# Sums made by accumulating transfers instead of by GpSimd and VectorE

## The chip, the cores and the metric

The kernel runs on one core of a Trainium2 chip. The metric is the device time of one execution in microseconds, the median of several runs. The engines are TensorE (PE in the profile; its weight loads PEld), VectorE (DVE), ScalarE (ACT), GpSimd (POOL) and SyncE (SP); the last three also issue transfers (DMA), each on a queue of its own that runs in order. Matrix products go from SBUF to PSUM; the other engines take them from PSUM.

## The reference

One inference step of a one-layer streaming encoder with 1024 prompt tokens and 64 sample tokens, model width 1024, all in float32:

```python
xn = rms_norm(x, g_attn)
rq, rk, rv, rg, sq, sk, sv, ga, gb = split(xn @ w_in)
A = rms_norm(retention(rope(rq), rope(rk), rv)) * silu(rg) @ w_ret_out
B = sliding_window_attention(sq, sk, sv, bias, sinks) @ w_swa_out
x += (sigmoid(ga) * A + sigmoid(gb) * B) @ w_mix_out
x += cross_attention(rms_norm(x, g_cross), memory)
x += (silu(rms_norm(x, g_ffn) @ w_gate) * (rms_norm(x, g_ffn) @ w_up)) @ w_down
y = rms_norm(x, g_final)
```

Three pieces matter here. The token norms need, for each of 1088 tokens, the sum of squares over 1024 features. The rotary turn makes from two halves a, b of a head the rows a cos - b sin and b cos + a sin. And nearly all large products are formed by Strassen's scheme in Winograd's form.

## The kernel before

**Layout.** Activations lie with features on the 128 partitions and the 1088 tokens along the row, in two halves of 544. Each float32 operand is split in two parts (a rounded one by a ScalarE cast, L125, the remainder by a VectorE subtraction, L126), and a product takes three matmuls (high x high, high x low, low x high).

**Strassen.** `strassen` (L270) makes a two by two block product of two weight tiles with the activations: seven products P1, P2, P6, P5, P7, P3, P4 in that order on TensorE. Each product is 4 x 6 matmuls of 272 columns (3 x 6 where a weight tile has only 384 rows). Between them VectorE adds up what is common to several results (u2, u5, u3), and `emit` takes each of the four results. The call with `part` (last group of the down projection) leaves out P2 and P4; these are made by `finish` with the rest weights.

**Weights.** For each step a pair of raw tiles is loaded by SP (tag raw, one pair of buffers in all), and `weight_ops` (L169) makes seven operands of them: P1 = a11, P2 = a12, P7 = a11 - a21, P6 = a22 - P7, P5 = a21 + a22, P3 = a12 - P6, P4 = a22. The four sums are made in place in the raw tiles, on GpSimd (L186, L187, L189, L192), on VectorE in five steps of the down projection (`by`). Each operand is split into a weight buffer (tag wq): five of them during the projections, six later. A weight buffer comes free when its product is done; the raw tiles come free when P3 and P4 are split, and only then can SP load the next pair.

**Order.** The products follow one another on TensorE; a planner with a simulated timeline puts the instructions of every engine in order, except where `issue_after` or `in_order` binds them. Each engine and each DMA queue then runs its own list in order.

**Stages.** (1) Projections, to about 800 us: 27 Strassen steps after two plain products; between the products the steps of the retention run. `rotated` turns a head of queries or keys in emit (four multiplications with cos and sin on VectorE, two additions per half of the tokens, on VectorE for the first two heads, on GpSimd for the others), then stores it. `token_squares` (L517) loads the 16 half tiles of x again, squares them on ScalarE and adds them on VectorE (L528) into the row `rstd`; `token_roots` needs the result at the third step of the next key product. (2) Window attention, merging and cross attention, to about 1480 us. (3) Gate and up products, 21 Strassen steps. (4) Down projection in three groups of 6, 8 and 8 feature tiles; each group goes over the eight output tiles in pairs m = 0, 2, 4, 6; `add` (L1739) adds the results to y, the part from PSUM on VectorE (L1742), the part from SBUF on GpSimd or, in the five steps with `turns`, on VectorE (L1744). While a group ends, the operands of the next are loaded (hl, from d_op) and split. In the last group's last step the eight halves of the rest weights (`hr`) are loaded too. (5) `finish`: the rest products, the final norm and the stores.

## Time and profile before

| | before |
|---|---|
| median of 3 runs | 2199.45 us (2199.18 to 2199.67) |
| profiled execution | 2199.31 us |
| its span | 2197.5 us |
| TensorE busy | 2155.3 us, 98% |
| VectorE busy | 1596.9 us, 73% |
| ScalarE busy | 884.3 us, 40% |
| GpSimd busy | 649.6 us, 30% |
| moved by DMA | 291.86 MB |

All times in the profile are microseconds from the start of the span, unless marked ns. A group's row gives line, engine, operation, tiles (written <- read), shape and count, then the busy time in us and the mean of one in ns, then the idle time of the engine just before these instructions with what ended it. A row of a DMA group ends with the median time from issue to landing. A timeline row gives start, duration, engine, line and operation.

### The profile page before, as it was taken

To read this page: it belongs to the slowest core of one execution; us is meant where nothing else is said; L and a number is where in the kernel's file an instruction comes from. 1 tells how busy PE (TensorE), PEld (TensorE's weight loads), DVE (VectorE), ACT (ScalarE), POOL (GpSimd) and SP (SyncE) were. 2 spreads that over 40 slices of the span, in tenths; PEclk is the share of its full clock that TensorE was granted. 3 is DMA by queue.
4 is the path that set the end of the run, shared out by engine and by line. 5 is a ranking of instruction groups with operands and counts; after the bars stand their busy time and mean duration, and the time that the engine had idled before them with its cause. 6 is when DMAs were issued, how large, how long until landed. Compare 5 with 4: busy or idle time off the path is not lost.

```text
span 2197.5 us, 41612 instructions
## 1 busy us (share of the span) xinstructions
PE 2155.3 (98%) x16388; PEld 2104.3 (96%) x16388; DVE 1596.9 (73%) x2721; ACT 884.3 (40%) x1902; POOL 649.6 (30%) x484
## 2 busy tenths in 40 slices
PE   9999999999999998999999999999999999999988
PEld 9999999999999997889999999999999999999987
DVE  7798878767688668876545555768877767779776
ACT  6434343437444355653233433343223222335433
POOL 2224535352264112320000000016655555431121
PEclk9999999999999999999999999999999999999999
DMA  4533434343455485427443121413433232466332
GB/s 172 185 110 111 149 111 162 121 138 112 136 187 163 143 272 161 134 77 231 129 150 112 40 73 55 140 57 109 146 114 104 96 119 81 150 231 221 111 116 82
DMA packets 160981, 291.86 MB, mean 133 GB/s; under 512 B 21554, under 2 KB 90098, under 8 KB 160658
## 3 DMA queue, kind: packets, MB, share of 16 engines
q1 hardware_dynamic: 151074, 263.42, 37.1%
q0 software_dynamic: 5104, 17.44, 2.2%
q10 hardware_dynamic: 4608, 8.36, 1.0%
q8 instruction: 129, 2.11, 0.4%
q14 instruction: 66, 0.54, 0.1%
HBM read 197.99 MB, written 91.95 MB: 132 GB/s over the span
## 4 chain that ended last, share of the span: by engine, by line
PE 74%; DVE 12%; DMA 6%; issue 3%; ACT 3%; POOL 2%; SPq 0%; DVEq 0%; ACTq 0%; POOLq 0%
PE pq L208 14%; PE pq L211 13%; PE pq L209 13%; PE pd L152 7%; PE pd L154 7%; PE pd L153 7%; DVE wq L126 3%; PE pss L1168 1%; DVE stage L659 1%; DVE B L126 1%; DMA hl<-d_op 1%; DMA raw<-w_down 1%; ACT wq L125 1%; DVE u L277 1%; DMA qs<-d_qkv 1%
## 5 line engine op out<-in xcount | busy, mean ns | idle before, releaser
L126 DVE TENSOR_TENSOR wq<-raw,wq 128x512 fp32r<-128x512 f32 (+1 forms) x498 | 444.8, 899 | 159.4 <-ACT wq L125 157.5
L125 ACT CAST wq<-raw 128x512 fp32r<-128x512 f32 (+1 forms) x498 | 299.6, 612 | 567.3 <-PE pq L211 210.6
L208 PE MATMUL pq<-T,wq 128*128 128x272 f32 x1800 | 496.8, 294 | 13.9 <-ACT wq L125 9.6
L209 PE MATMUL pq<-T,wq 128*128 128x272 f32 x1800 | 491.2, 289 | 0.0
L208 PE MATMUL pq<-B,wq 128*128 128x272 f32 x1550 | 424.3, 292 | 0.5 <-DVE u L277 0.5
L209 PE MATMUL pq<-B,wq 128*128 128x272 f32 x1550 | 420.0, 288 | 1.1 <-DVE B L126 1.1
L211 PE MATMUL pq<-T,wq 128*128 128x272 f32 x1800 | 374.6, 289 | 0.0
L186 POOL TENSOR_TENSOR raw<-raw 128x512 f32<-128x512 f32 (+1 forms) x53 | 79.1, 1493 | 996.1 <-DVE rs_r L316 477.1
L208 PEld LDWEIGHTS pq<-T,wq 128*128 128x128 f32 x1800 | 341.8, 190 | 17.0 <-ACT wq L125 10.3
L209 PEld LDWEIGHTS pq<-T,wq 128*128 128x128 f32 x1800 | 345.1, 192 | 0.0
L211 PE MATMUL pq<-B,wq 128*128 128x272 f32 x1550 | 320.3, 287 | 0.0
L209 PEld LDWEIGHTS pq<-B,wq 128*128 128x128 f32 x1550 | 294.5, 190 | 1.3 <-DVE B L126 1.3
L208 PEld LDWEIGHTS pq<-B,wq 128*128 128x128 f32 x1550 | 291.6, 188 | 1.6 <-issue 1.4
L211 PEld LDWEIGHTS pq<-T,wq 128*128 128x128 f32 x1800 | 281.7, 190 | 0.2
L211 PEld LDWEIGHTS pq<-B,wq 128*128 128x128 f32 x1550 | 240.2, 188 | 0.0
L277 DVE TENSOR_TENSOR u<-pq,u 128x544 f32<-128x544 f32 x174 | 125.1, 719 | 64.7 <-PE pq L211 64.0
L189 POOL TENSOR_TENSOR raw<-raw 128x512 f32<-128x512 f32 (+1 forms) x53 | 75.3, 1421 | 95.5 <-DVE wq L126 91.3
L659 DVE TENSOR_TENSOR stage<-pq,u 128x544 f32<-128x544 f32 x108 | 77.5, 717 | 32.5 <-PE pq L211 21.5
L1196 POOL TENSOR_TENSOR t<-t,den 128x768 f32<-128x768 f32 (+2 forms) x34 | 49.6, 1460 | 126.7 <-DVE den L1194 40.3
L192 POOL TENSOR_TENSOR raw<-raw 128x512 f32<-128x512 f32 (+1 forms) x53 | 76.9, 1452 | 15.6 <-DVE wq L126 12.2
L187 POOL TENSOR_TENSOR raw<-raw 128x512 f32<-128x512 f32 (+1 forms) x53 | 78.1, 1474 | 3.4
L152 PE MATMUL pd<-xc,wq 128*128 128x256 f32 (+1 forms) x256 | 74.6, 291 | 0.3 <-DVE qf L1453 0.3
(411 smaller groups left out, 4742.3 us busy)
## 6 DMA issues: line engine op xcount, KB each, us to landing
hl<-d_op SPq DMA_DIRECT2D x84, 272.0 KB, 4.2
d_op<-stage SPq DMA_DIRECT2D x44, 272.0 KB, 2.3
d_op<-ht SPq DMA_DIRECT2D x44, 272.0 KB, 4.2
raw<-w_gate SPq DMA_DIRECT2D x22, 512.0 KB, 3.5
raw<-w_up SPq DMA_DIRECT2D x22, 512.0 KB, 4.9
raw<-w_down SPq DMA_DIRECT2D x16, 512.0 KB, 4.2
d_gate<-stage ACTq DMA_DIRECT2D x28, 272.0 KB, 2.5
d_qkv<-stage SPq DMA_DIRECT2D x24, 272.0 KB, 2.9
```

Source lines behind the costliest of these rows:

```text
L125: self.last_cast = self.nc.scalar.copy(hi, src).ins
L126: self.last_low = self.nc.vector.tensor_tensor(out=lo, in0=src, in1=hi.bitcast(F32), op=ALU.subtract).ins
L152: mm(ps, wh, xh, start=start, stop=False)
L153: mm(ps, wh, xl, start=False, stop=False)
L154: self.last_mm = mm(ps, wl, xh, start=False, stop=stop).ins
L186: tt(out=a11, in0=a11, in1=a21, op=sub)
L187: tt(out=a21, in0=a21, in1=a22, op=add)
L208: mm(ps[:, c, :HC], w[:, 0, ks], x[:, 0, cs], start=start, stop=False)
L209: mm(ps[:, c, :HC], w[:, 0, ks], x[:, 1, cs], start=False, stop=False)
L211: self.last_mm = mm(ps[:, c, :HC], w[:, 1, ks], x[:, 0, c * HC:(c + 1) * HC], start=False, stop=stop).ins
L277: add = lambda out, a, b: nc.vector.tensor_tensor(out=out, in0=a, in1=b, op=ALU.add)
L659: nc.vector.tensor_tensor(out=o, in0=ps, in1=sb, op=ALU.add)
```

## The change

1. `weight_ops`: the four sums of a step become transfers that add to their target, issued by GpSimd (`dma_start` with `accum_op`). Such a transfer can only add, so the operands change sign where the scheme subtracts: P7 = a11 + a21, P6 = P7 + a22, P5 as before, P3 = a12 + P6, and the sums behind the products subtract instead (`join` with a sign). This holds for all steps, so `by` goes.
2. `token_squares`: the additions become accumulating transfers, and the loop takes the two halves of the tokens in turn for each tile instead of one half after the other.
3. `rotated`: b sin is formed with its sign turned, and both additions become accumulating transfers, for all heads.
4. `add` of the down projection: all additions to y on VectorE.
5. The loads of the rest weights are bound behind the last load of the last pair of weights.

```diff
-        tt = (by or nc.gpsimd).tensor_tensor
+        def plus(out, x):
+            self.last_sum = nc.gpsimd.dma_start(out, x, accum_op=ALU.add).ins
+
         put("P1", a11)
         put("P2", a12)
-        tt(out=a11, in0=a11, in1=a21, op=sub)
-        tt(out=a21, in0=a21, in1=a22, op=add)
+        plus(a11, a21)
+        plus(a21, a22)
         put("P7", a11)
-        tt(out=a11, in0=a22, in1=a11, op=sub)
+        plus(a11, a22)
         put("P6", a11)
         put("P5", a21)
-        self.last_sum = tt(out=a12, in0=a12, in1=a11, op=sub).ins
+        plus(a12, a11)
         put("P3", a12)
         put("P4", a22)
...
-        add(u2, self.product(w, x, "P6", "T2"), u1)
-        add(u5, self.product(w, x, "P5", "T1"), u2)
+        self.join(u2, self.product(w, x, "P6", "T2"), u1, "b-p")
+        self.join(u5, self.product(w, x, "P5", "T1"), u2, "p-b")
         ps = self.product(w, x, "P7", "T3")
-        add(u3, ps, u2)
-        emit(1, 1, ps, u5)
-        emit(0, 1, self.product(w, x, "P3", "B22"), u5)
-        emit(1, 0, None if part else self.product(w, x, "P4", "T4"), u3)
+        self.join(u3, ps, u2)
+        emit(1, 1, ps, u5, "b-p")
+        emit(0, 1, self.product(w, x, "P3", "B22"), u5, "p-b")
+        emit(1, 0, None if part else self.product(w, x, "P4", "T4"), u3, "p-b")
+
+    def join(self, out, ps, sb, signs="p+b"):
+        a, b = (sb, ps) if signs == "b-p" else (ps, sb)
+        self.nc.vector.tensor_tensor(out=out, in0=a, in1=b, op=ALU.add if signs == "p+b" else ALU.subtract)
...
-        for t in range(2):
-            hs = slice(t * HALF, (t + 1) * HALF)
-            for k in range(KT):
-                x = self.ra.tile([P, HALF], F32, tag=tags[k % 4], bufs=1, name="xsq")
+        for k in range(KT):
+            for t in range(2):
+                hs = slice(t * HALF, (t + 1) * HALF)
+                x = self.ra.tile([P, HALF], F32, tag=tags[(2 * k + t) % 4], bufs=1, name="xsq")
                 self.load(x, self.io["xT"][k, :, hs])
                 acc = self.rstd[:, hs]
                 nc.scalar.activation(x if k else acc, x, AF.Square)
                 if k:
-                    nc.vector.tensor_tensor(out=acc, in0=acc, in1=x, op=ALU.add)
+                    nc.gpsimd.dma_start(acc, x, accum_op=ALU.add)
...
-                    tt(out=sb, in0=b, in1=sin, op=ALU.mult)
+                    nc.vector.scalar_tensor_tensor(sb, b, -1.0, sin, ALU.mult, ALU.mult)
                     tt(out=sa, in0=a, in1=sin, op=ALU.mult)
                     tt(out=a, in0=a, in1=cos, op=ALU.mult)
+                    nc.gpsimd.dma_start(a, sb, accum_op=ALU.add)
                     tt(out=b, in0=b, in1=cos, op=ALU.mult)
-                    add = (nc.vector if h < 2 else nc.gpsimd).tensor_tensor
-                    add(out=a, in0=a, in1=sb, op=ALU.subtract)
-                    add(out=b, in0=b, in1=sa, op=ALU.add)
+                    nc.gpsimd.dma_start(b, sa, accum_op=ALU.add)
...
             if ps is not None:
-                nc.vector.tensor_tensor(out=v, in0=ps, in1=v, op=ALU.add)
+                self.join(v, ps, v, "b-p" if signs == "b-p" else "p+b")
             if sb is not None:
-                by.tensor_tensor(out=v, in0=sb, in1=v, op=ALU.add)
+                self.join(v, v, sb, "p-b" if signs == "p-b" else "p+b")
...
                 if last and m == KT - 2:
                     rest_raws = []
-                    for i in range(KT):
-                        pool = self.more if i < 6 else self.hl
-                        rest_raws.append(pool.tile([P, HALF], F32, tag="hl", name="hr")[:, :n])
-                        load_half(rest_raws[i], i, f0 + g // 2, f0 + g)
+                    with self.tc.issue_after(self.loaded):
+                        for i in range(KT):
+                            pool = self.more if i < 6 else self.hl
+                            rest_raws.append(pool.tile([P, HALF], F32, tag="hl", name="hr")[:, :n])
+                            load_half(rest_raws[i], i, f0 + g // 2, f0 + g)
...
-                    w = self.weight_ops(raws, n, ("P2", "P4") if last else (), by)
+                    w = self.weight_ops(raws, n, ("P2", "P4") if last else ())
```

More of the change, by code (lines that the diff above doesn't have):

```diff
@@ L276, in strassen @@
         u1, u2, u3, u5 = (self.fp.tile([P, 2, HC], F32, tag=t, bufs=1, name=t) for t in ("u1", "u2", "u3", "u5"))
-        add = lambda out, a, b: nc.vector.tensor_tensor(out=out, in0=a, in1=b, op=ALU.add)
         ps = self.product(w, x, "P1", "B11")
@@ L658, in taken, with emit @@
                 else:
[L659 removed]
+                    self.join(o, ps, sb, signs)
                 return flat(o)
             def project(w, put, act=None, other=None):
[L663 to L664 removed]
+                def emit(i, t, ps, sb, signs="p+b"):
+                    o = taken(ps, sb, signs)
                     (nc.vector if act is not None else nc.gpsimd).tensor_tensor(
@@ L702, in values, with emit @@
             def values(w, h, by=self.strassen):
-                def emit(i, t, ps, sb):
-                    self.store(self.d_qkv[2, 2 * h + i, :, half(t)], taken(ps, sb))
+                def emit(i, t, ps, sb, signs="p+b"):
+                    self.store(self.d_qkv[2, 2 * h + i, :, half(t)], taken(ps, sb, signs))
                 by(w, self.ops, emit)
@@ L714, in emit @@
                         left.extend((2, 2))
-                    o, r = taken(ps, sb), self.rstd[:, half(t)]
+                    o, r = taken(ps, sb, signs), self.rstd[:, half(t)]
                     at, edge = (slice(0, 512), slice(512, HALF)) if t == 0 else (slice(32, HALF), slice(0, 32))
@@ L1647, in save, with gate @@
                 self.store(self.d_op[OPS.index(name), n], src)
-            def gate(i, t, ps, sb):
+            def gate(i, t, ps, sb, signs="p+b"):
                 g = gates[i, t]
                 if sb is not None:
-                    nc.vector.tensor_tensor(out=g, in0=ps, in1=sb, op=ALU.add)
+                    self.join(g, ps, sb, signs)
                     ps = None
@@ L1758, in load_half @@
         def load_half(tile, m, a, b):
-            self.load(tile.rearrange("p (k m) -> p k m", m=P), io["w_down"][m, :, a:b, :])
+            self.loaded = self.load(tile.rearrange("p (k m) -> p k m", m=P), io["w_down"][m, :, a:b, :])
         for gi, g in enumerate(GROUPS):
@@ L1764, in down, with emit @@
             for m in range(0, KT, 2):
-                turns = m == KT - 2 and not last or m in (0, 2) and gi > 0
-                by = nc.vector if turns else nc.gpsimd
-                def emit(i, t, ps, sb, m=m, by=by):
-                    add(m, i, t, ps, sb, by)
+                def emit(i, t, ps, sb, signs="p+b", m=m):
+                    add(m, i, t, ps, sb, signs)
                     if last and t == 1:
```

20 lines of the change are left out of this document (8 added, 12 removed).

## The prediction

> **What bounds the kernel now.** I read the page's first part, then a table of busy time by stretch, then the waits and the chain at the places where TensorE stands still.
>
> ```profile
> span 2197.5 us, 41612 instructions
> PE 2155.3 (98%) x16388; PEld 2104.3 (96%) x16388; DVE 1596.9 (73%) x2721; ACT 884.3 (40%) x1902; POOL 649.6 (30%) x484
> ```
>
> TensorE is busy for 98% of the span: 2197.5 - 2155.3 = 42.2 us is all that can be saved by feeding it better, apart from time at a lower clock. By stretch (start:end, length, busy time and count of each engine, granted clock, DMA share, GB/s):
>
> ```profile
> 70.00:120.00 50.00, 47.08 (x360) 46.64 (x359) 47.35 (x67) 20.96 (x36) 13.06 (x8) 0.96 0.52 171
> 800.00:900.00 100.00, 90.46 (x677) 74.69 (x675) 84.47 (x201) 62.77 (x225) 25.42 (x21) 0.98 0.60 189
> 1480.00:1920.00 440.00, 440.00 (x3507) 440.00 (x3506) 335.03 (x393) 132.94 (x225) 247.03 (x164) 1.00 0.34 113
> 1920.00:2000.00 80.00, 75.83 (x596) 74.81 (x595) 64.75 (x97) 32.29 (x63) 22.84 (x16) 1.00 0.64 218
> 2080.00:2120.00 40.00, 31.85 (x219) 31.41 (x218) 32.94 (x52) 14.35 (x25) 2.59 (x2) 0.87 0.51 160
> 2160.00:2197.50 37.50, 26.59 (x205) 25.59 (x203) 24.16 (x64) 10.24 (x24) 1.48 (x2) 0.87 0.34 120
> ```
>
> The reader is to see three things. In the gate and up products (1480 to 1920) TensorE never stands: 440 / 3507 = 0.1255 us a matmul, so a Strassen step of 7 products of 24 matmuls takes 168 x 0.1255 = 21.1 us, and nothing can be gained there, only lost. The idle time of 800 to 900 and of the tail lies where the diff changes nothing but the loads of the rest weights. What the change can reach is 2.9 us in 70 to 120, 4.2 in 1920 to 2000 and 8.2 in 2080 to 2120. Closer:
>
> ```profile
> 90.00:94.00 4.00, 1.72 (x14) 1.50 (x12) 4.00 (x8) 0.66 (x1) 0.00 (x0) 1.00 0.87 223
> 94.00:98.00 4.00, 3.92 (x22) 3.92 (x23) 2.94 (x6) 1.80 (x3) 0.00 (x0) 0.68 1.02 403
> 2085.00:2088.00 3.00, 0.28 (x3) 0.06 (x1) 3.00 (x6) 3.00 (x7) 0.00 (x0) 1.00 0.59 137
> 2088.00:2092.00 4.00, 3.89 (x19) 3.90 (x20) 4.00 (x7) 1.76 (x4) 0.00 (x0) 0.60 0.87 303
> 2104.00:2110.00 6.00, 0.97 (x8) 0.74 (x6) 6.00 (x11) 4.03 (x7) 0.00 (x0) 0.94 0.00 1
> 2110.00:2113.00 3.00, 2.71 (x12) 2.71 (x13) 3.00 (x6) 1.41 (x3) 0.00 (x0) 0.50 0.57 175
> 2113.00:2117.00 4.00, 4.00 (x22) 4.00 (x22) 0.99 (x2) 0.62 (x1) 0.00 (x0) 0.61 0.45 131
> ```
>
> In each gap VectorE is busy to the last tenth, and behind each gap the granted clock falls (0.68, 0.60, 0.50) for some microseconds, so a gap costs more than itself. For the last group, count the matmuls missing against one per 0.1255 us: 24 - 3, 32 - 19, 48 - 8, 24 - 12 and 32 - 22 are 96, or **12.0 us** for the two gaps. For the early one 32 - 14 and 32 - 22 are 28, or **3.5 us**. The chain of waits across the largest gap:
>
> ```profile
> 2098.02 5.27 DMA raw<-w_down
> 2103.32 0.69 DVE raw L186
> 2108.99 0.61 DVE raw L189
> 2110.29 0.59 PE pq L208
> ```
>
> A pair of weights is loaded late, because its only buffer is freed late; then come sum, split, sum, split, one behind the other.
>
> **The change part by part.** Its price is one number, D: the time from the issue of an accumulating transfer until it has landed. Each Strassen step forms four sums; L186, L189 and L192 depend on each other, with a split between the first two.
>
> ```profile
> L186 POOL TENSOR_TENSOR raw<-raw 128x512 f32<-128x512 f32 (+1 forms) x53 | 79.1, 1493 | 996.1 <-DVE rs_r L316 477.1 <-DVE wq L126 227.5 <-issue 52.1
> L189 POOL TENSOR_TENSOR raw<-raw 128x512 f32<-128x512 f32 (+1 forms) x53 | 75.3, 1421 | 95.5 <-DVE wq L126 91.3 <-DVE rv L1040 4.2
> L186 DVE TENSOR_TENSOR raw<-raw 128x512 f32<-128x512 f32 (+1 forms) x5 | 3.8, 757 | 5.5 <-DMA raw<-w_down 5.5
> L126 DVE TENSOR_TENSOR wq<-raw,wq 128x512 fp32r<-128x512 f32 (+1 forms) x498 | 444.8, 899 | 159.4 <-ACT wq L125 157.5
> d_qkv<-stage POOLq DMA_DIRECT2D x16, 272.0 KB, 2.7
> d_gate<-stage POOLq DMA_DIRECT2D x20, 272.0 KB, 4.0
> d_gate<-stage POOLq DMA_DIRECT2D x3, 272.0 KB, 2.4
> L699 POOL DMA_DIRECT2D d_qkv<-stage x8 | 4.4, 551 | 0.4 <-POOL stage L696 0.4
> raw<-w_gate SPq DMA_DIRECT2D x22, 512.0 KB, 3.5
> raw<-w_down SPq DMA_DIRECT2D x16, 512.0 KB, 4.2
> hr<-w_down SPq DMA_DIRECT2D x8, 256.0 KB, 3.0
> ```
>
> *D.* The trace has no accumulating transfer and none from SBUF to SBUF. Nearest are plain transfers that GpSimd issues: 272 KB land after 2.4 us where the DMA engines are quiet (the three of 676 to 692 us), after 2.7 and 4.0 in the median of two groups. A sum also reads its target; 256 KB more cost 3.5 - 3.0 = 0.5 us between two loads. The bounds are 2.4 (the second read is hidden) and 4.0 (it meets traffic as d_gate does). I take 2.4 + 0.5 = **2.9 us**, since the sums come behind their own load, when the engines have little else. The Trainium skill (DMA: Bandwidth & Descriptors, "Anatomy of one DMA — SWDGE (gpsimd) path") gives about 2.0 us fixed plus bytes over 436 GB/s: 2.6 for 256 KB, 3.2 if both reads count. The rows (2.4 to 2.7 for 272 KB) agree with it for one read; by 3.2, an estimate from that page, the last group below would gain 3 x 0.9 = 2.7 us less.
>
> *Weight sums in steady state (232 of them; 53 x 4 leave GpSimd, 5 x 4 VectorE).* Each costs 2.9 instead of 1.45 us, so the third product's weight (P6, behind two sums) comes about 3 us later. Cover, from one step of the gate and up products:
>
> ```profile
> 1765.83 1.29 POOL L186 TENSOR_TENSOR raw<-raw 128x512 f32<-128x512 f32 x1 [4.24 <-DMA raw<-w_up]
> 1770.10 1.29 POOL L189 TENSOR_TENSOR raw<-raw 128x512 f32<-128x512 f32 x1
> 1771.42 0.62 ACT L125 CAST wq<-raw 128x512 fp32r<-128x512 f32 x1 [3.55 <-POOL raw L189]
> 1772.08 1.23 DVE L126 TENSOR_TENSOR wq<-raw,wq 128x512 fp32r<-128x512 f32 x1 [0.51 <-ACT wq L125]
> 1785.28 0.72 DVE L277 TENSOR_TENSOR u<-pq,u 128x544 f32<-128x544 f32 x1 [0.75 <-PE pq L211]
> ```
>
> The split of P6 ends at 1773.3; L277 takes its product at 1785.28, which began 24 x 0.1255 = 3.0 earlier, at 1782.3: 9.0 us of cover, and 3 are used. What must also hold is the loop through the one pair of raw buffers: load, split of P1, sum, split of P7, sum, sum, split of P3, next load. With 0.62 + 0.90 = 1.5 a split and 4.2 the load it is 4.2 + 4.5 + 3D = 8.7 + 3D, 17.4 at D = 2.9, below 21.1. Cost **0**; the cover is gone at D = 4.1. GpSimd's queue now waits for a landing before nearly each issue; behind it stand the gates' second products (L1656) and the operand differences (L1671 to L1680), which the up products and the stores want within a step, so some three waits of 2.9 us are hidden by 21.1. The projections have five weight buffers instead of six, so their weights are split later and have less cover: bounds 0 and 6 (what two sums cost more, 3 us, at two of their steps), I take **+1**, near zero, since side work between their products stretches the steps.
>
> *Weight sums in the down projection.* Group 0 has 384 columns instead of 512: 126 x 0.1255 = 15.8 us a step against a loop of 16.9 (0.5 us less in loads and splits): up to 1.1 x 3 = 3.3; none if the traffic moved off GpSimd pays it. I take **+2**. Group 1 has 21.1 us a step: 0. The last group leaves out two products, 120 x 0.1255 = 15.1 us a step against 17.4: three steps lose 2.3 each, 7 us. Against that stand the 12.0 us above. They should go: of the chain's links from 2103 on, VectorE's own sums and its queue make most, and it loses those sums (four a step) while the y additions of these steps were on it already. 7.0 - 12.0 = **-5.0**; bounds by D: 2.4 gives 0.8 x 3 - 12.0 = -9.6, 4.0 gives 5.6 x 3 - 12.0 = +4.8.
>
> *Squares and turns.*
>
> ```profile
> L528 DVE TENSOR_TENSOR rstd<-rstd,xsq 128x544 f32<-128x544 f32 x14 | 11.8, 846 | 0.1
> L695 DVE TENSOR_TENSOR stage<-stage,stage 128x544 f32<-128x544 f32 x8 | 5.7, 718 | 0.0
> 110.90 0.72 DVE L528 TENSOR_TENSOR rstd<-rstd,xsq 128x544 f32<-128x544 f32 x1
> 122.50 0.22 DVE L314 TENSOR_SCALAR rs_v<-pt 128x8 f32<-128x8 f32 x2
> ```
>
> VectorE loses 11.8 us of squares and, with L696 alike, 11.4 us of turns, most of it in a stretch where it is full (47.35 of 50). The early gap of 3.5 us should close: **-3.5**, bounds -3.5 and +5 (the transfers stand in GpSimd's one queue before the weight sums of two steps, a D each less 0.4). The two chains of seven transfers take 7 x 2.9 = 20.3 us if they overlap, begin at 71 and are wanted at 122.5: covered by some 30 us. SP's stores of turned rows wait a D longer, with weight loads behind them on its queue: 0, or one D, inside that bound, where such a load is the last thing a step waits for.
>
> *y additions on VectorE* (20 of L1744, 1.53 us on GpSimd, 0.72 where VectorE makes them already): 14.4 us more, 20 weight sums fewer; off the path, **0**. *Rest weights last*: six of the eight now go out ahead of a pair that TensorE waits for, and pass its queue and its DMA engines.
>
> ```profile
> 2088.59 8.52 SPq L119 DMA_DIRECT2D hr<-w_down  x6
> ```
>
> At that pace eight take 8 x 1.4 = 11.4 us and land 3.0 later, 14.4, behind the last pair, and are wanted when the last step's 15.1 us are through: **0**, up to +3 if that cover is short; the pair's load of 5.27 us may come down to the median of 4.2, which is inside the last group's term.
>
> Sum: +1 + 2 - 5.0 - 3.5 = -5.5. The profiled execution took 2199.31 us, 1.8 over its span and 0.14 under the median of the runs (2199.45). 2199.3 - 5.5 = **2193.8 us**.
>
> **The rivals.** *Slower: the loop through the raw buffers outlasts a step.* Place: every step of the down projection, then the gate and up products; it decides from D = 4.1 there. At D = 4.0 group 0 loses (20.2 - 15.8) x 3 = 13, the last group loses 4.8, the projections 3, and the early part gains 2: +19, 2218. Each 0.1 us beyond 4.1 adds 0.3 x 20 = 6 in the gate and up products. For it: d_gate's 4.0 us, and a DMA share of 0.64 in 1920 to 2000. Against: 2.4 us in quiet, and a share of 0.34 where most steps are. Chance 0.28. *Slower: GpSimd's queue.* Fourteen transfers of 2.9 us, each waiting for the one before, are 41 us of a queue that holds the sums of the first steps: +5 early instead of -3.5, and 2202; for it, that the queue runs in order; against, that two chains alternate. Chance 0.06. *No change*: D = 3.3. The last group gains 12.0 - 3.5 x 3 = 1.5, group 0 loses 4 of the 6.9 that its loop asks for, the projections 1.5, early -3.5: +0.5, 2199.8. Chance 0.17. *The change does not do what it says*: the planner's order leaves the early sums behind squares or the rest weights where they were; then the last group keeps its gaps, 2199 to 2205; chance 0.04.
>
> **How the numbers follow.** The forecast (0.45) has its own range from D = 2.4 (-9.6 - 3.5 = -13, 2186) to 3.2 (2197). A measurement of this kernel tells about 0.2%, 4.4 us, from no change. Faster by more: 0.41, the forecast without its upper end; within: that end, 0.04, the no-change case and a little of the last, 0.22; slower: the two slower rivals and the rest, 0.37. The range takes the forecast's low end with the tail of tighter loops and the slower rival up to D = 4.1: 2184 to 2222.
>
> **What would show it.** The raw tile's accumulating transfers, issue to landing: 2.9 us right, above 4.1 wrong. 2085 to 2117 without a gap over 3 us and a clock of 1.00. 90 to 98 with 60 matmuls or more. 1480 to 1920 still 440 of 440; one missing tenth there says that the loop, not the product, sets the pace, and then the prediction is wrong by twenty times that. On GpSimd a row for the issue near 0.55 us.

## The result and the profile after

The changed kernel takes **2354.84 us** in the median of 4 runs (2351.97 to 2355.87), the kernel before 2199.56 us beside it: a ratio of 1.0705, with a 95% interval from 1.0689 to 1.0721. The forecast was 2193.8 us with a range to 2222. The profiled execution took 2355.21 us, its span is 2353.4 us.

The first part of the page, the row of GpSimd's DMA queue (packets, MB, share of the 16 engines), and the chain by engine:

```profile
span 2353.4 us, 42055 instructions
PE 2199.1 (93%) x16388; PEld 2137.3 (91%) x16388; DVE 1472.6 (63%) x2691; ACT 879.6 (37%) x1902; POOL 520.4 (22%) x514
...
q0 software_dynamic: 45136, 90.30, 20.1%
...
PE 31%; DMA 19%; DVE 8%; issue 5%; ACT 3%; POOL 1%; SPq 0%; POOLq 0%; ACTq 0%; DVEq 0%
```

VectorE's busy time fell by 1596.9 - 1472.6 = 124.3 us and GpSimd's by 129.2 (the sums took it 309.4 us by the rows of before, L186 to L192; their issues take 201.7 below). Of VectorE's 124.3 us only some 24 are work that left it, an estimate from the rows of before: 11.8 of squares, 11.4 of turns, 20 sums of 0.76, less 14.4 of y additions that came. The rest is that what stayed got shorter: L126, 498 times in both kernels, has a mean of 899 ns before and 785 now. In the kernel without transfers, told below, GpSimd adds again, L126 has 892 ns and VectorE 1598.2 us. So VectorE's instructions are longer where GpSimd adds, which I had not counted. TensorE, 98% busy before, is 93% busy now: it stands still for 154.3 us instead of 42.2. Work was taken from two engines that had time, and what was put in its place keeps the one waiting that had none. The groups that say why:

```profile
L125 ACT CAST wq<-raw 128x512 fp32r<-128x512 f32 (+1 forms) x498 | 295.9, 612 | 787.4 <-DMA raw<-raw 508.7
L183 POOL DMA_DIRECT2D raw<-raw x232 | 201.7, 869 | 1381.1 <-DVE rs_r L320 477.0
L126 DVE TENSOR_TENSOR wq<-raw,wq 128x512 fp32r<-128x512 f32 (+1 forms) x498 | 387.1, 785 | 420.3 <-ACT wq L125 418.6
```

and the first of them before:

```profile
L125 ACT CAST wq<-raw 128x512 fp32r<-128x512 f32 (+1 forms) x498 | 299.6, 612 | 567.3 <-PE pq L211 210.6
```

The casts of the weight operands on ScalarE wait 508.7 us for accumulating transfers; before, the largest of these waits, 210.6 us, was for TensorE to free a weight buffer. And the issue of an accumulating transfer keeps GpSimd for 0.869 us, where the issues of plain ones (L699 before) had 0.551. The transfers themselves, issue to landing, beside the loads:

```profile
raw<-raw POOLq DMA_DIRECT2D x220, 256.0 KB, 3.4
...
raw<-w_up SPq DMA_DIRECT2D x22, 512.0 KB, 5.1
stage<-stage POOLq DMA_DIRECT2D x32, 272.0 KB, 5.5
...
rstd<-xsq POOLq DMA_DIRECT2D x14, 272.0 KB, 5.5
```

So D, the price on which the forecast rested, is 3.4 us for a weight sum: above the 2.9 taken, but inside the bounds of 2.4 and 4.0. Squares and turns take 5.5. Four stretches (start:end, length, busy time and count by engine, granted clock, DMA share, GB/s), in this order: gate and up products; early; from the last up product into group 0; from the end of group 1 into the last group.

```profile
1600.00:2000.00 400.00, 373.81 (x2895) 369.64 (x2896) 245.59 (x310) 99.74 (x173) 166.20 (x137) 0.98 0.56 143
100.00:150.00 50.00, 28.60 (x205) 27.75 (x204) 21.24 (x44) 12.49 (x22) 14.52 (x17) 0.78 0.90 210
2060.00:2110.00 50.00, 40.77 (x308) 38.84 (x307) 36.05 (x58) 15.76 (x30) 6.03 (x7) 1.00 0.86 279
2221.00:2284.00 63.00, 51.73 (x364) 51.07 (x363) 41.26 (x65) 21.64 (x38) 9.42 (x11) 0.89 0.63 154
```

The gate and up products, where before TensorE was busy in 440 of 440 us, now lose a fifteenth (373.81 of 400 us). To place the loss, I use one event of every Strassen step: ScalarE's copy of P1's product (u<-pq, 58 in each kernel). The table gives the time between the copies of the first and last step named, in us, as differences of starts rounded to a tenth; the three columns at the right are experiments told below (no accumulating transfer at all; weight sums alone by transfers; squares and turns alone).

| stretch | before | after | no transfers | weight sums only | squares, turns only |
|---|---|---|---|---|---|
| start to 1st key step | 61.4 | 61.0 | 61.8 | 61.3 | 61.2 |
| to 1st window-query step (4 steps) | 100.7 | 131.0 | 98.8 | 105.5 | 113.9 |
| to 1st gate column (11 steps) | 323.4 | 347.3 | 325.5 | 330.2 | 334.3 |
| gate columns (11 steps) | 297.4 | 321.7 | 299.0 | 319.8 | 298.7 |
| window, merging, cross attention | 701.6 | 710.7 | 702.1 | 707.6 | 702.8 |
| gate and up, 1st to last up step (20 steps) | 424.7 | 478.4 | 424.2 | 478.9 | 424.5 |
| down: to the last group | 179.2 | 184.3 | 176.5 | 186.4 | 176.7 |
| last group (3 steps) | 56.9 | 61.6 | 53.4 | 64.1 | 54.2 |
| last step and finish | 52.1 | 57.3 | 53.6 | 54.5 | 52.0 |

Of 156 us, 54 are lost in the gate and up products, where I had put 0; 30 in the first four steps, where I had put -3.5; and 48 in the rest of the projections. The other 24 lie in the last rows and in the window stretch; the 9.1 of the window stretch were not traced.

**One period of the loop, gate and up products.** From the timeline of after (start, duration, engine, line, operation), the rows on which the pair of raw tiles depends:

```profile
1772.62 0.90 POOL L183 DMA_DIRECT2D raw<-raw  x1 [5.56 <-DMA raw<-w_gate]
...
1776.34 0.86 POOL L183 DMA_DIRECT2D raw<-raw  x1 [2.82 <-DMA raw<-raw]
...
1776.69 0.69 DVE L126 TENSOR_TENSOR wq<-raw,wq 128x512 fp32r<-128x512 f32 x1 [4.87 <-ACT wq L125]
...
1777.79 0.85 POOL L183 DMA_DIRECT2D raw<-raw  x1 [0.59 <-DVE wq L126]
...
1781.60 0.85 POOL L183 DMA_DIRECT2D raw<-raw  x1 [2.96 <-DMA raw<-raw]
...
1786.42 1.88 DVE L1664 TENSOR_TENSOR stage<-stage,stage 128x544 f32<-128x544 f32 x1
1786.52 0.33 SPq L119 DMA_DIRECT2D raw<-w_up  x1
...
1787.68 1.84 POOL L1678 TENSOR_TENSOR ht<-stage 128x544 f32<-128x544 f32 x1
...
1788.22 1.84 DVE L126 TENSOR_TENSOR wq<-raw,wq 128x512 fp32r<-128x512 f32 x1
...
1790.09 0.76 SPq L119 DMA_DIRECT2D raw<-w_up  x1
...
1796.20 0.88 POOL L183 DMA_DIRECT2D raw<-raw  x1 [4.91 <-DVE u L292]
```

From the first sum of one pair (1772.62) to that of the next (1796.20) are 23.58 us: 5.17 to the third sum (a transfer and the split of P7), 3.81 to the fourth (a transfer), 4.92 to the load of the first raw tile (a transfer and the split of P3), then 3.57 until the split of P4 has freed the second, since its subtraction (1788.22) stands behind a multiplication of the up branch (L1664) on VectorE. Both are slow while GpSimd forms operand differences (L1678 and its neighbours): the subtraction takes 1.84 us, and 0.69 at 1776.69, where GpSimd only issues. Then come 6.11 until the second tile has landed (1795.53) and GpSimd issues again. Three transfers at 3.4 are 10.2; the other **13.4** are what I had called 8.7. The step itself is 21.1. This is the working of one period; in the mean of 16 steps of after a step takes 374.6 / 16 = 23.4 us.

**The early gap.** GpSimd's timeline around it, ScalarE's cast, and the wait of TensorE between 60 and 160 us:

```profile
108.22 0.86 POOL L532 DMA_DIRECT2D rstd<-xsq  x1 [1.36 <-issue]
116.06 0.88 POOL L532 DMA_DIRECT2D rstd<-xsq  x1 [6.98 <-DMA rstd<-xsq]
116.77 1.06 POOL L183 DMA_DIRECT2D raw<-raw  x1
117.56 1.16 POOL L699 DMA_DIRECT2D stage<-stage  x1
120.51 0.86 POOL L532 DMA_DIRECT2D rstd<-xsq  x1 [1.79 <-issue]
...
125.21 0.86 POOL L699 DMA_DIRECT2D stage<-stage  x1 [0.49 <-issue]
127.79 0.86 POOL L532 DMA_DIRECT2D rstd<-xsq  x1 [1.72 <-issue]
129.26 0.87 POOL L183 DMA_DIRECT2D raw<-raw  x1 [0.62 <-issue]
130.77 0.87 POOL L183 DMA_DIRECT2D raw<-raw  x1 [0.63 <-issue]
...
137.57 0.88 POOL L183 DMA_DIRECT2D raw<-raw  x1 [3.12 <-DMA raw<-raw]
```

```profile
137.19 1.14 ACT L125 CAST wq<-raw 128x512 fp32r<-128x512 f32 x2 [13.78 <-DMA raw<-raw]
```

```profile
PE pq L209 <- ACT wq L125: 29.2, 3, 20.3
```

The sum of 116.77 went out right behind a square (L532) that had waited 6.98 us for the transfer before it. Between that sum and the next two (129.26, 130.77) stand six other transfers, four of turns (L697, L699) and two of squares, and P6's cast had its sum at 137.19. TensorE stood for up to 20.3 us.

### The profile page after: what moved, and what is told of

It is laid out like the page before. It is cut to its first block, busy times and chain, and to the rows that moved or that the text cites. A ratio compares the mean times of both kernels' runs of the same rounds, so it can differ in the third digit from the quotient of the medians.

```text
span 2353.4 us, 42055 instructions
## 1 busy us (share of the span) xinstructions
PE 2199.1 (93%) x16388; PEld 2137.3 (91%) x16388; DVE 1472.6 (63%) x2691; ACT 879.6 (37%) x1902; POOL 520.4 (22%) x514
## 3 DMA queue, kind: packets, MB, share of 16 engines
q0 software_dynamic: 45136, 90.30, 20.1%
## 4 chain that ended last, share of the span: by engine, by line
PE 31%; DMA 19%; DVE 8%; issue 5%; ACT 3%; POOL 1%; SPq 0%; POOLq 0%; ACTq 0%; DVEq 0%
DMA raw<-raw 12%; PE pd L152 7%; PE pd L154 6%; PE pd L153 6%; DVE wq L126 3%; DMA raw<-w_up 2%; ACT wq L125 2%; PE pq L209 2%; PE pq L210 2%; DMA raw<-w_gate 2%; PE pq L212 2%; DMA raw<-w_down 1%; PE pss L1171 1%; POOL raw L183 1%; DVE T L126 1%
## 5 line engine op out<-in xcount | busy, mean ns | idle before, releaser
L126 DVE TENSOR_TENSOR wq<-raw,wq 128x512 fp32r<-128x512 f32 (+1 forms) x498 | 387.1, 785 | 420.3 <-ACT wq L125 418.6
L209 PE MATMUL pq<-T,wq 128*128 128x272 f32 x1800 | 512.2, 302 | 90.9 <-ACT wq L125 72.7
L125 ACT CAST wq<-raw 128x512 fp32r<-128x512 f32 (+1 forms) x498 | 295.9, 612 | 787.4 <-DMA raw<-raw 508.7
L183 POOL DMA_DIRECT2D raw<-raw x232 | 201.7, 869 | 1381.1 <-DVE rs_r L320 477.0
L210 PE MATMUL pq<-T,wq 128*128 128x272 f32 x1800 | 502.7, 296 | 0.0
L209 PEld LDWEIGHTS pq<-T,wq 128*128 128x128 f32 x1800 | 354.1, 197 | 99.5 <-ACT wq L125 91.0
L212 PE MATMUL pq<-T,wq 128*128 128x272 f32 x1800 | 379.6, 294 | 9.1 <-DVE wq L126 9.1
L210 PEld LDWEIGHTS pq<-T,wq 128*128 128x128 f32 x1800 | 356.4, 198 | 0.0
L212 PEld LDWEIGHTS pq<-T,wq 128*128 128x128 f32 x1800 | 287.7, 194 | 10.2 <-DVE wq L126 10.1
L292 DVE TENSOR_TENSOR stage<-pq,u 128x544 f32<-128x544 f32 x144 | 103.4, 718 | 65.7 <-DMA d_qkv<-stage 38.8
L292 DVE TENSOR_TENSOR u<-pq,u 128x544 f32<-128x544 f32 x116 | 82.5, 719 | 29.8 <-PE pq L212 29.2
L152 PE MATMUL pd<-xc,wq 128*128 128x256 f32 (+1 forms) x256 | 74.6, 291 | 0.3 <-DVE qf L1456 0.3
L154 PE MATMUL pd<-xc,wq 128*128 128x256 f32 (+1 forms) x256 | 74.3, 290 | 0.0
L153 PE MATMUL pd<-xc,wq 128*128 128x256 f32 (+1 forms) x256 | 73.9, 289 | 0.0
L1193 ACT ACTIVATE t<-t,nm 128x192 f32<-128x192 f32 (+2 forms) x136 | 58.9, 434 | 36.3 <-DVE nm L1188 36.1
```

The costliest lines, as they stand in the source:

```text
L125: self.last_cast = self.nc.scalar.copy(hi, src).ins
L126: self.last_low = self.nc.vector.tensor_tensor(out=lo, in0=src, in1=hi.bitcast(F32), op=ALU.subtract).ins
L152: mm(ps, wh, xh, start=start, stop=False)
L153: mm(ps, wh, xl, start=False, stop=False)
L154: self.last_mm = mm(ps, wl, xh, start=False, stop=stop).ins
L183: self.last_sum = nc.gpsimd.dma_start(out, x, accum_op=ALU.add).ins
```

## The experiments

In the expectations the four weight sums go by line numbers of several kernels: L186 is the first sum (a11 takes a21), L187 the second (a21 takes a22), L190 the third (a11 takes a22), L193 the fourth (a12 takes a11). Below they are sums 1 to 4. Three theories stood at the start: A, the loop through the one pair of raw tiles; B, squares and turns ahead of the sums in GpSimd's queue; C, the traffic itself, by the byte. "The 16 steps" are those between the up steps of pairs 1 and 9, read from the copies of P1.

### No accumulating transfer

```diff
-            self.last_sum = nc.gpsimd.dma_start(out, x, accum_op=ALU.add).ins
+            self.last_sum = (by or nc.gpsimd).tensor_tensor(out=out, in0=out, in1=x, op=ALU.add).ins
...
-                    nc.gpsimd.dma_start(acc, x, accum_op=ALU.add)
+                    nc.vector.tensor_tensor(out=acc, in0=acc, in1=x, op=ALU.add)
...
-                    nc.gpsimd.dma_start(a, sb, accum_op=ALU.add)
+                    add(out=a, in0=a, in1=sb, op=ALU.add)
```

> All accumulating transfers are taken out again: squares and turns are added by VectorE and GpSimd, weight sums by GpSimd's (in a few steps VectorE's) additions, as before; the turned sign, the y additions on VectorE and the order of the rest weights stay. If the transfers are the whole cause of the loss, this is 2199 within 8 us, and the gate and up products take 425 us again between the first and the last up step. If the sign, the y additions or the order of the rest weights had a part, it stays above 2210. My prediction had these parts at 0.

Measured: 2194.05 us, ratio to before 0.9975 (0.9965 to 0.9985); gate and up products 424.2 us. The transfers are the whole loss, and what is left of the change (signs, order of the squares, y additions, rest weights) is a small gain: 2354.8 - 2194.1 = 160.8 us are theirs.

### Weight sums alone, squares and turns alone

Against after, the first has the two lower pieces of the diff above and the second its upper one. First the weight sums alone:

```diff
-                    nc.gpsimd.dma_start(acc, x, accum_op=ALU.add)
+                    nc.vector.tensor_tensor(out=acc, in0=acc, in1=x, op=ALU.add)
...
-                    nc.gpsimd.dma_start(b, sa, accum_op=ALU.add)
+                    add(out=b, in0=b, in1=sa, op=ALU.add)
```

> Only the weight sums go by transfers; squares and turns are added by the engines as before. Theory A (the loop through the one pair of raw buffers, fixed part 13.3 us plus three transfers of 3.4, is longer than a step of 21.1 us): the gate and up products keep their +54 us. Theory B (squares and turns stand in GpSimd's queue ahead of the sums of the first steps): the first four steps of the projections come back by some 30 us, so about 2300 to 2320 in all. Theory C (traffic: each transfer costs by its bytes, wherever it is): the loss falls only by the share of the squares and turns in the transfers, 46 of 278, to about 2330.

Measured: 2311.16 us, ratio 1.0504 (1.049 to 1.0518). The gate and up products keep their +54 (theory A); the first four steps come back by 25.5 us (theory B). The fall of 44 us is larger than the share of the transfers asks for.

Squares and turns alone:

```diff
-            self.last_sum = nc.gpsimd.dma_start(out, x, accum_op=ALU.add).ins
+            self.last_sum = (by or nc.gpsimd).tensor_tensor(out=out, in0=out, in1=x, op=ALU.add).ins
```

> Only squares and turns go by transfers; the weight sums are GpSimd's additions again. Theory A: the gate and up products are back at 425 us, and so is the down projection. Theory B: GpSimd's queue still holds the sums of the first steps behind the squares and turns, so the first four steps of the projections lose 20 to 30 us and the whole is 2220 to 2235. Theory C: 46 of 278 transfers, so about 2225 too, but spread over the projections rather than in the first steps. If neither squares nor turns cost anything without the sums' transfers, 2200.

Measured: 2222.51 us, ratio 1.0108 (1.0092 to 1.0123): +28.5 against no transfers, by the table 15.1 in the first four steps and 8.8 in the eleven behind them; nothing in the gate and up products. Less than expected in the first steps: squares and turns cost there with the sums' transfers more than without, and 117.1 + 28.5 = 145.6 leaves 15 us that only all together cost.

### Squares or turns alone

The kernel without transfers, with one of them put back; the squares:

```diff
-                    nc.vector.tensor_tensor(out=acc, in0=acc, in1=x, op=ALU.add)
+                    nc.gpsimd.dma_start(acc, x, accum_op=ALU.add)
```

> Of the transfers only the 14 of the squares' sums are left; turns and weight sums are the engines' additions. If GpSimd's in-order queue is what they cost (theory B: weight sums of the first steps stand behind squares that wait for their loads), the loss of the squares and turns together between the second and the fourth step (q0 to q1, +14 us against the kernel without transfers) stays: 2204 to 2210. If the turns caused that, it is 2194 to 2197.

Measured: 2199.57 us, ratio 0.9999 (0.9988 to 1.0011), which is 5.5 over no transfers and between the two cases. The stretch that the expectation names (q0 to q1, from the second to the fourth step) takes 46.6 us without transfers, 61.2 with squares and turns, and 52.0 with the squares alone: a part of the loss stays, not all of it.

The turns:

```diff
-                    add(out=a, in0=a, in1=sb, op=ALU.add)
-                    add(out=b, in0=b, in1=sa, op=ALU.add)
+                    nc.gpsimd.dma_start(a, sb, accum_op=ALU.add)
+                    nc.gpsimd.dma_start(b, sa, accum_op=ALU.add)
```

> Of the transfers only the 32 of the turns are left; squares and weight sums are the engines' additions. The run with squares and turns lost 12 us between the third and the last pair of key and query steps, where no squares are left: the turns' own share, by the stage tiles that are held a transfer longer and by sums behind them in GpSimd's queue. Expected 2204 to 2212, with q0 to q1 near its 46.6 us without transfers.

Measured: 2219.95 us, ratio 1.0086 (1.0062 to 1.011): 26 us over no transfers, twice what was expected, and the larger part of the pair. The stretch from q0 to q1 takes 51.8 us and not some 46.6, as expected, so each of the two costs 5 there, and both together 15. Two waits of VectorE's additions into the stage tiles name the place; from the waits of 120 to 440 us, and from the timeline:

```profile
DVE stage L292 <- DMA d_qkv<-stage: 28.9, 5, 7.9
```

```profile
275.70 0.72 DVE L292 TENSOR_TENSOR stage<-pq,u 128x544 f32<-128x544 f32 x1 [7.95 <-DMA d_qkv<-stage]
```

Without transfers the same wait is 7.0 us there, in three. A turned row lands 5.2 us after its issue, then it is stored, and only then is its stage tile free; VectorE's next addition stands and waits, with all that is behind it. That the held tile, and not GpSimd's queue, is the cause was read from the waits, not tested.

### Two pairs of raw buffers

Weight sums by transfers, and in the gate and up products a second pair of raw tiles:

```diff
-                more = self.temp.enter_context(self.tc.tile_pool(name="hl2", bufs=6, reuse_waits="tile", side="right"))
...
+                self.wps = [self.temp.enter_context(self.tc.tile_pool(name="raws2", bufs=2, reuse_waits="tile", side="right")), self.wp]
...
-            raw = self.wp.tile([P, 1024], F32, tag="raw", bufs=2, name="raw")
+            raw = wp.tile([P, 1024], F32, tag="raw", bufs=2, name="raw")
```

> Weight sums by transfers alone, and from the second up product to the ninth pair two pairs of raw buffers take turns instead of one; nothing else differs from the run with the weight sums alone. Theory A: two steps share the loop of 23.5 us and more, so the gate and up products fall back from 478 to 425 to 432 us. Theory C (bytes) or a theory by which the engines' queues are held by their waits for transfers: 470 to 480 us stays.

Measured: 2279.22 us, ratio 1.0356 (1.034 to 1.0371). Its 16 steps take 348.5 us; they take 375.8 with one pair and 334.6 without transfers. Of 41.2 us the second pair gives back 27.3, two thirds. The gate and up products as a whole take 450.9, where A had 425 to 432. Theory C is out, since no byte less was moved, but A explains only a part. (In this kernel the pool hl2 is opened later, at the last pair.)

### Which of the four sums

Two of the sums by transfers, the other two by GpSimd's additions (squares and turns by the engines from here on):

```diff
-        plus(a11, a21)
+        add(a11, a21)
         plus(a21, a22)
...
-        plus(a11, a22)
+        add(a11, a22)
...
         plus(a12, a11)
```

This is the pair of sums 2 and 4. In every kernel of this section `plus` is the transfer and `add` the engines' addition.

> Two of the four weight sums go by transfers, L187 (a21 takes a22) and L193 (a12 takes a11); L186 and L190 are GpSimd's additions; squares and turns on the engines. One of the two transfers (L193) lies on the loop through the raw pair. Theory A: the loop is 13.3 + 3.4 + 2 x 1.4 = 19.5 us, shorter than the 20.9 us of a step, so the stretch from the second to the tenth up step (16 steps; 334.6 us with no transfers, 375.8 with all four) is 335 to 338 us. Theory C (each transfer costs by its bytes or by its issue): half of the 41 us, so 355.

Measured: **2184.80 us**, ratio 0.9933 (0.9909 to 0.9957), the fastest kernel of this study; 333.0 us for the 16 steps. As theory A said.

The pair of sums 1 and 3:

```diff
         plus(a11, a21)
-        plus(a21, a22)
+        add(a21, a22)
...
         plus(a11, a22)
...
-        plus(a12, a11)
+        add(a12, a11)
```

> The other two of the four weight sums go by transfers, L186 (a11 takes a21) and L190 (a11 takes a22), both on the loop through the raw pair, with the split of P7 between them; L187 and L193 are GpSimd's additions. Theory A: the loop is 13.3 + 2 x 3.4 + 1.4 = 21.5 us, 0.6 above a step, so the stretch of 16 steps is 344 us, some 10 above the one with no transfers, and more than with the other two sums. Theory C: half of the 41 us, 355, the same as with the other two.

Measured: 2302.57 us, ratio 1.0466 (1.0441 to 1.0491); 382.1 us for the 16 steps. Half of the transfers, the same size, the same bytes: the one half costs nothing, the other as much as all four. Theory C is out for good. A had the sign, but gave 344. The two rows for their 16 steps, sums 2 and 4 first:

```profile
1529.00:1862.00 333.00, 333.00 (x2655) 333.00 (x2654) 236.18 (x288) 96.20 (x162) 167.67 (x129) 1.00 0.47 138
```

```profile
1565.80:1947.90 382.10, 349.56 (x2696) 342.81 (x2695) 251.01 (x289) 92.91 (x161) 173.08 (x129) 0.99 0.42 120
```

The DMA engines are busier (0.47) and move more per second (138 GB/s) where nothing is lost. So four more kernels, with one sum or another pair. Of the four lines, `plus` stays only for sum 1 (a11 takes a21), sum 3 (a11 takes a22), sums 1 and 4, and sum 4 (a12 takes a11); sum 1 as the example:

```diff
         plus(a11, a21)
-        plus(a21, a22)
+        add(a21, a22)
...
-        plus(a11, a22)
+        add(a11, a22)
...
-        plus(a12, a11)
+        add(a12, a11)
```

> Only L186 (a11 takes a21, the first sum) goes by a transfer; everything else is added by the engines. Theory A with the loop as the run with L186 and L190 shows it (22.8 us a step, of which 14.5 are neither sum nor transfer): with one transfer 14.5 + 3.5 + 2 x 1.3 = 20.6 us, just below a step of 20.9, so the stretch of 16 gate and up steps is 335 to 340 us. Theory P (no loop; what counts is that the weight of the third product, P6, waits behind L186 and L190, and each transfer there costs its own share): half of the 47 us that the two cost together, about 358.

> Only L190 (a11 takes a22, the third sum) goes by a transfer. Theory A: one transfer on the loop, 335 to 340 us for the 16 steps. Theory P: about 358, as with L186 alone.

> L186 and L193 (the first and the last sum) go by transfers. Both lie on the loop through the raw pair, but only L186 lies ahead of the third product's weight. Theory A: two transfers on the loop, 14.5 + 7.0 + 1.3 = 22.8 us a step, so 360 to 382 us for the 16 steps, as with L186 and L190. Theory P: no more than with L186 alone.

> L193 alone (a12 takes a11, the last sum) by a transfer. If every link of the loop through the raw pair counts by its length, L193 costs as L190 did, some 15 us in the 16 steps (350 us). If the split behind L193 (P3) waits for its weight buffer anyway, which the last product of the step before frees, L193 costs nothing there: 333 to 336 us, and 2185 to 2194 in all.

| sums by transfer | median us | ratio (95%) | 16 steps |
|---|---|---|---|
| none | 2194.05 | 0.9975 (0.9965 to 0.9985) | 334.6 |
| 1 | 2252.79 | 1.0238 (1.0209 to 1.0267) | 363.7 |
| 3 | 2238.14 | 1.0171 (1.0141 to 1.0201) | 349.9 |
| 4 | 2189.58 | 0.9949 (0.9932 to 0.9966) | 333.3 |
| 1 and 4 | 2246.50 | 1.0209 (1.0182 to 1.0236) | 356.6 |
| 2 and 4 | 2184.80 | 0.9933 (0.9909 to 0.9957) | 333.0 |
| 1 and 3 | 2302.57 | 1.0466 (1.0441 to 1.0491) | 382.1 |
| all | 2311.16 | 1.0504 (1.049 to 1.0518) | 375.8 |

Theory A as I had it, links that may grow until their sum passes 21 us, falls: sum 1 alone, with a computed loop of 20.6, costs 29 us. The costs nearly add (29.1 + 15.3 = 44.4 against 47.5), so there was next to no slack for these two. Sum 4 lies on the same loop and costs nothing, alone or with sum 1, as the second case of its own expectation said. Theory P fits all of this in kind, except for its claim that there is no loop, which the next two runs test. What tells sum 1 and 3 from 2 and 4 is what stands behind them: the split of P7 behind 1, then sum 3, then the split of P6, each the next thing in line, while the split behind sum 2 (P5) comes after P6's, and that behind sum 4 (P3) comes last but one.

Where there was slack shows in the waits of the casts, for a product that frees their weight buffer or for a transfer; for the 16 steps before, with sum 1 by transfer, and with sum 4:

```profile
ACT wq L125 <- PE pq L211: 82.7, 37, 5.4
```

```profile
ACT wq L125 <- DMA raw<-raw: 93.4, 15, 9.0
...
ACT wq L125 <- PE pq L215: 9.3, 3, 5.6
```

```profile
ACT wq L125 <- PE pq L215: 68.8, 35, 5.4
...
ACT wq L125 <- DMA raw<-raw: 17.9, 6, 4.2
```

Before, many weights were split as soon as a buffer came free, and the split waited for TensorE. With sum 1 slow this is turned round: the casts wait for the transfer. With sum 4 slow it stays as before, 68.8 us in 35 waits for a product and 17.9 in 6 for a transfer. In one step sum 4 is issued at 1747.60 and has landed at 1750.92, and P3's cast starts only at 1752.37, when a product has freed its buffer:

```profile
1752.37 0.62 ACT L125 CAST wq<-raw 128x512 fp32r<-128x512 f32 x1 [2.34 <-PE pq L215]
```

So the loop has slack at its end, where P3's split waits for its buffer anyway, and next to none at its start, where sums 1 and 3 stand.

### Is it the raw pair?

The kernels with sum 1, and with sums 1 and 3, by transfer, each with the second pair of raw tiles from above. Theory E comes in here: the queues of ScalarE and VectorE are held at the splits of P7 and P6 until the transfers have landed, whatever raw tiles there are.

```diff
+                self.wps = [self.temp.enter_context(self.tc.tile_pool(name="raws2", bufs=2, reuse_waits="tile", side="right")), self.wp]
...
-            raw = self.wp.tile([P, 1024], F32, tag="raw", bufs=2, name="raw")
+            raw = wp.tile([P, 1024], F32, tag="raw", bufs=2, name="raw")
```

> L186 alone by a transfer (363.7 us for the 16 steps with one raw pair), with two pairs of raw buffers. Theory A: 334 to 337 us. Theory E: 350 to 364.

> L186 and L190 by transfers, as in the run that took 382 us for the 16 gate and up steps, and two pairs of raw buffers that take turns in these steps. Theory A (the loop through the one raw pair): 334 to 340 us. Theory E (ScalarE's and VectorE's in-order queues are held at the splits of P7 and P6 until the transfers have landed, whatever raw buffers there are): it stays at 365 to 382. In between: both have a part, as the 348 us of all four transfers with two pairs suggest.

Measured: sum 1 with two pairs takes 333.2 us for the 16 steps (363.7 with one), 2217.81 in all, ratio 1.008 (1.006 to 1.01). All of its 29 us come back, and TensorE is whole again; the 23.8 us by which this kernel is still over no transfers lie outside these steps. Sums 1 and 3 with two pairs take 352.6 (382.1 with one), 2272.60 in all, ratio 1.0329 (1.0307 to 1.0351). There 29.5 of 47.5 us come back. One pair and two, for sum 1:

```profile
1544.50:1908.10 363.60, 348.84 (x2691) 344.59 (x2691) 251.28 (x288) 93.32 (x161) 182.25 (x129) 0.98 0.37 115
```

```profile
1544.50:1877.70 333.20, 333.07 (x2653) 332.85 (x2652) 254.03 (x288) 93.99 (x161) 183.74 (x129) 1.00 0.39 121
```

So in the gate and up products the loop through the one raw pair is shown for sum 1, and for two thirds of what sums 1 and 3 cost together. The other 18 us stay with two pairs. In that kernel the casts still wait for transfers, and GpSimd too:

```profile
ACT wq L125 <- DMA raw<-raw: 147.8, 30, 7.3
...
POOL raw L183 <- DMA raw<-raw: 89.3, 30, 4.8
```

Theory E, queues held in order, would fit these waits, but they don't show it: with sum 1 and two pairs the casts wait for transfers too (69.7 us, 14 times) and TensorE loses nothing. What makes the 18 us is open.

### The rest weights alone

The kernel before, with the last part of the change:

```diff
-                    for i in range(KT):
+                    with self.tc.issue_after(self.loaded):
+                        for i in range(KT):
```

> The kernel before with one change: the loads of the rest weights are issued behind the last pair of w_down. My prediction had this at 0, up to +3. The kernel without any accumulating transfer, which also has the y additions on VectorE, is 0.25% faster than before; if that comes from the order of the rest weights, this run is 2193 to 2196 and the last three steps take 53.4 us instead of 56.9; if from the y additions, it is 2198 to 2202.

Measured: 2197.26 us, ratio 0.9988 (0.9976 to 1.0): between the two cases. The last three steps take 55.3 us, 56.9 before and 53.4 without transfers. The interval holds everything from no gain to the whole 0.25%, so the two parts are not told apart.

## Why the prediction was wrong, point by point

**D.** 3.4 us for the weight sums, 2.9 forecast: half a microsecond, inside the bounds. The Trainium skill (DMA: Bandwidth & Descriptors, "Anatomy of one DMA — SWDGE (gpsimd) path") gives about 2.0 us plus bytes over 436 GB/s. An estimate from it is 2.6 us for 256 KB, and 3.2 with the bytes counted twice for the second read; the measured median lies 0.2 over the latter, and no run shows that the second read is the reason. By the forecast's own formula 3.4 would have given 8.7 + 10.2 = 18.9, still below 21.1. The price was not the error.

**Weight sums in steady state: 0 forecast, +54 in the gate and up products.** The step that failed is "8.7 + 3D". The part without transfers measured 13.4. I had left out that the second raw tile comes free only with P4's split, behind that of P3 on VectorE's in-order queue (3.57 us), that its load counts from there (6.11 to the next sum, not 4.2), and some 0.4 us from landing to issue at each link. With 13.4 the cover is gone at D = 2.6, not 4.1: even at the 2.9 taken, the loop would have been 22.1. This puts the loss on the right loop, but no such sum of links gives its size: sum 1 alone cost 29 us where the working gives none, and sum 4 cost none. My rival of the slower loop (0.28) had the mechanism, but by its threshold, 4.1, this D cost nothing here. The "9.0 us of cover" for P6 was read from one step, and is a stock that a loop without slack uses up; by the experiments there was next to none for sums 1 and 3. Two pairs of raw tiles gave back all that sum 1 cost and two thirds of what all four cost; the cause of the last third is open.

**Projections: +1 forecast, +32 for the sums alone** (755.5 against 723.3 from the first key step to the last gate column). The step that failed is the bound of 6, what two sums cost more at two of the steps, with +1 taken because side work stretches the steps. Most of it, 20.8, lies in the eleven gate-column steps, where neither squares nor turns are about. Whether a second raw pair would give it back there was not tried, so that the same loop is the cause there is not shown.

**Down projection.** Group 0: +2 forecast, 35.2 to 44.9 us, +9.7. Group 1: 0 forecast, +0.6. (From the last up step to the last group it is only +5.1, as the passages between the groups got shorter.) Last group: -5.0 forecast, +4.7. The gaps did not go: instead of the two in before, 2.8 and 5.3 us, there are four, of 3.2, 4.7, 3.3 and 5.1, and all four wait for a cast of weights. The step that failed is that the gaps would go once VectorE's own sums had left its queue. Without transfers the stretch is 3.5 us shorter than before, so a part of the 12.0 us could be had, but by other parts of the change.

**Squares and turns: -3.5 forecast, +28.5 alone.** The early gap was to close as VectorE gets time. VectorE got time (21.24 of 50 us busy) and TensorE got 28.60 of 50. The failed step is the bound of +5: I counted one D per step for the queue, but in the queue stand transfers that wait for one another and for their loads, and each holds what is behind it. The rival of GpSimd's queue (0.06) was right in kind: with the sums' transfers the first four steps lose 32 us against no transfers. For the turns I priced SP's stores, and not the stage tiles, which are held one transfer longer; the run with the turns alone lost 26 us; that the held tiles are the reason was read from the waits, not tested.

**y additions and rest weights: 0 and 0 forecast.** Together, in the kernel without transfers, they gain 5.5 us (ratio 0.9975). This kernel also has the turned sign and the new order of the squares, and the parts are not told apart.

**The issue on GpSimd**, 0.55 forecast, took 0.87.

**What was right.** D within its bounds, the direction of VectorE's and GpSimd's relief (VectorE's was some five times what the moved work asks for), and the sentence that one missing tenth between 1480 and 1920 would say that the loop sets the pace.

## What to carry to other kernels

Before an operation is moved to a transfer, follow its target all the way round, from the load over the sums and splits until the buffer is loaded again, with every instruction that stands ahead in each in-order queue; the sum of the links that one can name is not enough (sum 1 alone cost 29 us where the sum was below a step), and a busy engine at the end of the loop hides how little slack there is. The same transfer costs nothing where the next operation on its target comes late or waits for something else anyway (sums 2 and 4: 0.67% faster than before, of which 0.25% come with the other parts of the change). It costs where a split stands right behind it (sums 1 and 3: 4.7% slower): in the gate and up products 29.1 / 16 = 1.8 us a step for sum 1 and 1.0 for sum 3, where the transfer lasts 3.4 us and GpSimd's addition 1.3. So sort the candidates by what stands behind them, not by what they take off an engine.

## What the hardware showed that was not expected

- An accumulating transfer of 256 KB within SBUF landed 3.4 us after its issue in the median with all four sums, 3.3 and 3.4 with two of them; of 272 KB in the crowded first stage 5.0 to 5.6 us (DMA share 0.90 from 100 to 150 us). Its issue keeps GpSimd for 0.87 to 0.89 us, a plain one for 0.55.
- GpSimd's queue has 45136 packets with 90.30 MB instead of 5104 with 17.44 MB, so 278 accumulating transfers added 40032 packets, 144 each, of 1.8 KB in the mean; the plain ones before have 3.4.
- VectorE's subtraction of 128 x 512 (L126) has a mean of 899 ns where GpSimd makes the weight sums and 785 where transfers make them, at the same count of 498. In one period it took 1.84 us beside GpSimd's operand differences and 0.69 without.
- Where the loop was too long, half of what TensorE lost did not show as a gap: with sum 1 by transfer its busy time for the 16 steps was 348.84 instead of 334.50, at a clock of 0.98 instead of 1.00, and only 14.8 of 29 us were idle (363.6 - 348.84).
